# One list schedule for both phases up to the branch, second-phase pools laid over the first's one by one, and the adaLN gate summed piece by piece

## The chip, the core and the metric

The kernel runs on one core of one Trainium2 chip. The core has five engines with an instruction queue each: TensorE (PE, matrix products), VectorE (DVE), ScalarE (ACT), GpSimd (POOL) and SyncE (SP, which here only issues transfers between memory and the core). They run side by side and wait for each other through semaphores. The metric is the device time of one execution in microseconds (us); the time of a kernel is the median of its runs.

## The reference

One decoder layer on a sequence of 4096 tokens with 1024 features. The input is normalised and modulated by an adaLN vector that is computed from a condition `c`, goes through one combined input projection into three mixers, and their outputs go through one output projection, a second norm, the adaLN gate and the residual:

```python
def _hybrid_layer(x, c_act, ada_w, ada_b, ...):
    shift, scale, gate = jnp.split(c_act @ ada_w + ada_b, 3, axis=-1)
    h = _rmsnorm(x, g_pre) * (1.0 + scale[:, None]) + shift[:, None]
    proj = h @ w_in
    aq, ak, av, ag, rkv, rg, gq, gkk, gv, gg = jnp.split(proj, ...)
    attn = _sliding_window_attention(aq, ak, av, sinks)      # 8 heads, 2 kv heads, window 128, sinks, ALiBi
    attn = attn * jax.nn.silu(ag)
    rkv = rkv + (_shift(rkv) - rkv) * mu_rkv
    rr, rk, rv = jnp.split(rkv, 3, axis=-1)
    rwkv = _rwkv7_mixer(h, rr, rk, rv, ...) * jax.nn.silu(rg)   # 4 heads, delta-rule state
    gla = _gla_mixer(h, gq, gkk, gv, ...) * jax.nn.silu(gg)     # 4 heads, chunks of 64
    y = jnp.concatenate([attn, rwkv, gla], axis=-1) @ w_out
    return x + gate[:, None] * _rmsnorm(y, g_post)
```

`shift` and `scale` are needed before the first token, `gate` only in the output stage.

## The kernel before

The sequence is cut into 16 supertiles of 256 tokens (`NT = 256`, `NS = 16`), and the program has two phases.

**Phase 1** computes the norm, the modulated h (kept as an fp16 pair of high and low part, `hT`, which is also written out to `hscr`), the GLA mixer and the RWKV-7 mixer; their outputs go to `mscr`. Per supertile it is written as generators: `stage_a` (norm, h), `stage_p` (GLA values, `pv`, and the low-rank gates, `lp`), `stage_d`, `stage_r`, `stage_k`, `stage_v` (the RWKV projections, all called `zz`), `stage_qa`, `stage_qb` and `stage_qc` (GLA products, and the RWKV triangular system) and `stage_q2`. In the triangular system `atp` holds products of RA and KB; they go through memory (`adr` to `AS`), a loop of 15 steps on VectorE (`tsc`, `TT`) inverts blocks, the result goes through memory again (`tdr` to `td`), and `Xp`, `Xq`, `X` on PE finish it into `tf`. `stage_q2` is serial: four chunks, each of `rp`, `rs`, `up`, `UV`, `sp`, `yp` and the state `Sst`, then the normalised `ysb` is transposed (`yt`). `stage_c` rewrites the weights of the second phase as high and low halves (`wscr`, `woscr`) along the way.

`stage_g` sums the gate, `silu(c) @ ada_w` for its 1024 columns. It takes 16 pieces of 128 x 4 x 128 numbers (256 KB each): SP loads a piece into the tile `hf`, GpSimd multiplies it by the condition (`scol`) and adds it up into `acc`, PE sums the partitions (`gp2`, two products of 512 columns), and the row goes to `gscr`. It is gated on the last supertile's `stage_a` and `stage_d`.

**Phase 2** is sliding attention, gates, output projection and residual. Its weights are seven pairs q0 to q6 of `wscr` (q0, q1 the queries, q2 keys and values, q3 to q6 the silu gates, products `gp` into `ag`). `stage_w` loads them, `stage_first` runs `qkv(0)`, `gates(0)`, `qkv(1)`, `stage_s(0)` is the attention of supertile 0 (scores `sc`, softmax `pr`, `ovp`), and `load_o` brings in the output weights. Then the program reads a flag, and all engines go through a branch (L1910) to a fallback that runs only if a GLA gate grew too large. After the branch come `stage_s` 1 to 15 and the output stages. Two transfers matter in the tail: `q5h` to `q6l` (weights) and `vscr`/`v_` (values of the attention).

**What sets the order.** Every instruction goes through a helper, `Lane.call` (L320, so almost every row of the profile bears this line), which records it as a step with a cost in a table of dependences. `Order.pin()` is a list scheduler over the recorded steps: it takes, engine by engine, the step that can start first, by a rank that is the place of its recording, moved by `LAG` and `URGENT`, and then fixes each engine's order by dependences. Recording order itself comes from `streams`, a list of generators with ranks, run by `emit`. `pin()` is called once, after phase 1. The steps of phase 2 up to the branch are recorded afterwards, and stand behind it in an order that follows their own priorities; which of them move in between phase 1's last steps is decided by buffers and priorities, not by the scheduler. The pools of phase 2 are allocated after phase 1's are given back, in one piece of memory.

Of the kernel before, what the change touches and what calls it, by code (L numbers as in the profile page):

```python
# [21 lines left out]
P = 128  # L22
D = 1024
T = 4096
NT = 256
NS = T // NT
# [3 lines left out]
LN2 = math.log(2.0)  # L30
GATE_LIMIT = 30.0
HOP, VL, AL, PL = 0.4, 0.2, 0.2, 0.06
EXP_TABLE, LN_TABLE = 1, 2
# [13 lines left out]
class Pool:  # L47


    def __init__(self, pool, bufs, held):  # L50
        self.pool, self.bufs, self.held = pool, bufs, held

    def tile(self, shape, dt, bufs=None, **kw):
        t = self.pool.tile(shape, dt, **kw) if bufs is None else self.pool.tile(shape, dt, bufs=bufs, **kw)
        self.held[t.tensor.name] = self.bufs if bufs is None else bufs
        return t

# [7 lines left out]
class Order:  # L65
# [3 lines left out]
    def __init__(self, tc):  # L69
        self.tc, self.held, self.masks, self.lag, self.urgent = tc, {}, {}, 0, 0  # L70
        self.steps = []
        self.wrote, self.read, self.users, self.slots, self.known = {}, {}, {}, {}, set()

    def pool(self, pool, bufs=1):
        return Pool(pool, bufs, self.held)

# [22 lines left out]
    def note(self, eng, name, outs, ins, func, r):  # L99
# [21 lines left out]
        elif e == "SP":  # L121
            st.bytes = math.prod(ins[0].shape) * SIZE[ins[0].dtype]
            kb = st.bytes / 1024
            st.occ = 0.47
            st.lat = next((t for k, t in ((8, 1.9), (32, 2.0), (128, 2.3), (256, 2.6), (512, 3.5)) if kb <= k), 4.8)
# [84 lines left out]
    def forget(self):  # L210

        self.steps = []
        for table in (self.wrote, self.read, self.users):
            table.clear()

    def pin(self):
# [167 lines left out]
def hybrid_kernel(ctx, tc, x, vecs, rows, adaw, w1, wl, w2, wo, w2aug, a2, gk2, cst, ctr, ctg, abias, out):  # L384
    nc = tc.nc
# [6 lines left out]

    def pool_of(at, name, bufs=1, **kw):
        return model.order.pool(at.enter_context(tc.tile_pool(name=name, bufs=bufs, **kw)), bufs)

# [87 lines left out]

    wa = pool_of(ctx, "wa", 1)
    sp_ = pool_of(ctx, "shared", 1)

# [137 lines left out]
    with ExitStack() as p1:  # L624

        wk1 = [pool_of(p1, f"work1{n}", 1) for n in "abcd"]
        pp = pool_of(p1, "c1p", 1)
        order = (("hf", "gl", "b1", "zs", "gw", "cgc", "bl", "gk1s", "zl0", "zl1", "zl2", "ch", "cl", "cs"),
                 ("zb0", "zb1", "zb2", "ta", "ep", "em", "b2", "KB"),
# [341 lines left out]
        def stage_g(_):  # L971

            yield [("a", NS - 1), ("w", NS - 1)]
            for g in range(2):
                acc = wt([P, 4, P], "acc", 1, tag="gw")
                for n in range(4):
                    for h in range(2):
                        aw = wt([P, 4, P], "hf", 2)
                        SP.dma_start(aw, adaw[8 + 2 * g + n // 2, :, 4 * h : 4 * h + 4, (n % 2) * P : (n % 2 + 1) * P])
                        yield [aw]  # L980
# [528 lines left out]

        streams((9, "l", stage_l, None), (11, "g", stage_g, None))  # L1510
        for i in range(NS):
# [10 lines left out]
    w2k, pp, wg, w2m, w2p, w2o, wb = [pool2(n) for n in ("work2k", "c2p", "wg", "work2m", "work2p", "work2o", "wb")]  # L1522
    pools = {"q": w2k, "kT": w2k, "vt": w2k, "v4": w2k, "mxa": w2m, "mxb": w2m, "pr": w2p, "yv": w2o, "sm1": w2o}

# [56 lines left out]
    def qkv(i):  # L1581
# [25 lines left out]
        for n in range(2):  # L1607
# [42 lines left out]
    def stage_s(i):  # L1650
# [3 lines left out]
        q, kT, v4 = f["q"], f["kT"], f["v"]  # L1654
        yield [q, kT, "at", "sq"]

        vblk = [F[i - 1]["v"][1] if i > 0 else None, *v4]
        mx = f["mx"] = wt([P, 4, NT], "mxa", 2)
        for a in range(2):
# [4 lines left out]
            for jp in range(2):  # L1664
                for kv in range(2):
                    sc = pst(("at", "sq")[kv], "sc").rearrange("p (j n) -> p j n", j=2)
                    for jj in range(2):
# [8 lines left out]
                if jp == 0:  # L1676
                    yield ["at", "sq"]
            nm = st.tile([P, 8], F32, tag="nm", name="nm")
# [20 lines left out]
            for kv in range(2):  # L1699
# [8 lines left out]
            ov = [pst(tag, "ovp")[:, 0:P].rearrange("p (j n) -> p j n", j=4) for tag in tags]  # L1708

# [10 lines left out]
            for n in range(4):  # L1720
                S.copy(mx[:, 0:4, a * P + 32 * n : a * P + 32 * n + 32], ov[n])
            yield ["at", "sq"]

# [166 lines left out]
    for t, n in tiles_o:  # L1890
        load_o(t, n)


    flag = nc.values_load(fi[0:1, 0:1], min_val=0, max_val=1)
# [157 lines left out]
```

## Time and profile before

| what | value |
|---|---|
| median of 3 runs | 2154.26 us (2151.35 to 2157.72) |
| profiled execution, its own time | 2149.78 us |
| its span | 2148.0 us |
| mean granted clock of TensorE | 0.988 |
| instructions | 59214 |
| GpSimd busy | 199.9 us (9%) |

Read the profile like this: first which engine is busy through the span, then where its digit falls, then the waits in these places, then what the releaser was doing at that time. A supertile of phase 1 takes some 62 us, and phase 2 begins in earnest at the branch at about 1165 us.

### The profile page before, as it was taken

The numbers are of one execution on the slowest core, as the hardware profiler recorded it, in microseconds if no ns is written. First come the engines' busy times: TensorE is split into PE (matmuls) and PEld (weight loads), VectorE is DVE, ScalarE is ACT, GpSimd is POOL, SyncE is SP. The second block draws the span as 40 slices with busy tenths as digits, with TensorE's granted clock in tenths as the row PEclk, the third lists the DMA queues.
The fourth block names the chain that finished last, engine by engine and source line by source line (L and its number), as shares of the span: only waits on it lengthen the run. The fifth ranks groups of instructions, "written<-read, shape, count | busy, mean of one in ns | idle before, by whom it ended". The sixth has DMA issues, their size and how long they took to land. (4 is left out here: it accounts for less than half of the span.)

```text
span 2148.0 us, 59214 instructions
## 1 busy us (share of the span) xinstructions
PE 2037.3 (95%) x23735; PEld 1600.4 (75%) x23735; DVE 1626.2 (76%) x5204; ACT 1144.5 (53%) x2741; POOL 199.9 (9%) x404
## 2 busy tenths in 40 slices
PE   4999999999999999999878999999999999999996
PEld 4778878888888887777657667777777777777773
DVE  6677677787777689887756888777778877777876
ACT  3966666667676667754324444434344444444442
POOL 0011111110111110112700000000000000000000
PEclk9999999999999999999989999999999999999998
DMA  9232322232323134422515343433343333334341
GB/s 316 91 108 82 93 77 84 71 96 84 120 78 107 42 108 123 126 83 62 172 53 179 128 160 106 135 103 111 115 135 121 121 121 111 115 115 141 110 132 69
DMA packets 187243, 241.80 MB, mean 113 GB/s; under 512 B 52160, under 2 KB 145874, under 8 KB 182740
## 3 DMA queue, kind: packets, MB, share of 16 engines
q1 hardware_dynamic: 185220, 236.76, 34.1%
q8 instruction: 188, 3.08, 0.6%
q10 hardware_dynamic: 1744, 1.21, 0.2%
q14 instruction: 91, 0.75, 0.1%
HBM read 177.08 MB, written 60.82 MB: 111 GB/s over the span
## 5 line engine op out<-in xcount | busy, mean ns | idle before, releaser
L320 PEld LDWEIGHTS <-mtp 128*128 128x128 f16 x1344 | 130.7, 98 | 143.9 <-issue 5.1
L320 PE MATMUL op<-o,mtp 128*128 128x512 f16 x768 | 174.2, 380 | 0.0
L320 ACT ACTIVATE pr<-pr,nm,lsc 128x256 f32<-128x256 f32 (+1 forms) x256 | 149.2, 585 | 38.6 <-DVE nm L320 38.6
L320 PE MATMUL op<-ov,mtp 128*128 128x512 f16 x576 | 146.0, 384 | 2.1 <-ACT mtp L320 2.1
L320 PEld LDWEIGHTS <-hT 128*128 128x128 f16 x1536 | 117.4, 99 | 22.9 <-issue 4.4
L320 DVE TENSOR_TENSOR yv<-op,yv 128x512 f32<-128x512 f32 x112 | 75.2, 683 | 57.6 <-PE op L320 40.6
L320 DVE CUSTOM_DVE_ANT_0 pr<-sc,ab,sinks 128x256 f32<-128x256 f32 (+1 forms) x256 | 108.1, 476 | 13.3 <-PE sc L320 8.4
L320 ACT ACTIVATE mtp<-yv,oi 128x1024 f16<-128x1024 f32 x32 | 36.6, 1144 | 126.3 <-DVE yv L320 124.8
L320 ACT ACTIVATE ag<-gp,gh 128x512 f32<-128x512 f32 x64 | 43.7, 682 | 108.2 <-PE gp L320 108.2
L320 PE MATMUL pv<-gvh,hT 128*128 128x272 f16 x512 | 99.8, 284 | 1.4 <-DVE kg L320 1.3
L320 DVE SCALAR_TENSOR_TENSOR ag<-ag,gp 128x512 f32<-128x512 f32 x64 | 43.8, 684 | 71.4 <-ACT ag L320 71.3
L320 POOL COPY kT<-kT 128x512 f16<-128x512 f16 x15 | 9.8, 652 | 896.5 <-DVE kT L320 896.5
L320 PE MATMUL zz<-hT,kh 128*128 128x256 f16 x512 | 92.7, 273 | 0.0
L320 PE MATMUL qp<-hT,q1h 128*128 128x256 f16 x512 | 88.9, 277 | 2.7 <-issue 2.3
L320 PE MATMUL gqk<-hT,gqkh 128*128 128x256 f16 x512 | 87.5, 273 | 4.0 <-DVE zb L320 3.3
L320 PE MATMUL zz<-hT,rh 128*128 128x256 f16 x512 | 89.5, 278 | 0.0
L320 PE MATMUL lp<-hT,Lh 128*128 128x256 f16 x512 | 89.3, 273 | 0.1
L320 PE MATMUL qp<-hT,q0h 128*128 128x256 f16 x512 | 85.4, 273 | 2.7 <-DVE ag L320 2.3
L320 PE MATMUL zz<-hT,vh 128*128 128x256 f16 x512 | 87.8, 273 | 0.0
L320 PE MATMUL gp<-hT,q3h 128*128 128x256 f16 x512 | 87.2, 276 | 0.1
L320 PE MATMUL gp<-hT,q5h 128*128 128x256 f16 x512 | 86.7, 273 | 0.0
L320 ACT ACT_TABLE_LOAD x65 | 83.4, 1283 | 5.3 <-DMA sinks<-in_rows 4.2
(428 smaller groups left out, 6146.8 us busy)
## 6 DMA issues: line engine op xcount, KB each, us to landing
ov<-woscr SPq DMA_DIRECT2D x96, 512.0 KB, 4.1
xt<-in_x SPq DMA_DIRECT2D x16, 1024.0 KB, 4.9
hscr<-hT SPq DMA_DIRECT2D x16, 1024.0 KB, 4.7
hT<-hscr SPq DMA_DIRECT2D x16, 1024.0 KB, 4.9
out<-yv SPq DMA_DIRECT2D x32, 512.0 KB, 2.9
x<-in_x SPq DMA_DIRECT2D x30, 512.0 KB, 3.9
cs<-in_w SPq DMA_DIRECT2D x112, 128.0 KB, 2.2
v<-vscr SPq DMA_DIRECT2D x128, 64.0 KB, 3.0
```

The costliest lines, as they stand in the source:

```text
L320: r = f(*args, **kw)
```

## The change

1. `pin()` is no longer called after phase 1 but after `load_o`, just ahead of the branch, so that phase 1, `stage_w`, `stage_first`, `stage_s(0)` and the loads of the output weights are one list schedule.
2. The second phase's pools are laid over the first's one by one. `Pool` knows its users, and the first use of a second-phase tile depends on every step that used the first-phase pools it lies on (`w2k` over pool a; `c2p` and `work2m` over a and b; `wg`, which holds q5 and q6, over b and c; `work2o` over b, c and d; `wb`, the output weights, over c, d and `c1p`). `work2p` (`pr`) becomes a pool of its own. The scratch for dynamic transfers is made smaller (`dynamic_dma_scratch_size=1024`).
3. `stage_g` has rank 0.5 instead of 11, four groups instead of two, each gated on the `stage_a` of supertile 4, 6, 8 or 10, with tiles of its own (`gaw`, one buffer, and `gac`). In the planner's cost its loads are 5 us later.
4. For `qkv(0)`, `qkv(1)` and `stage_s(0)` other PSUM banks are used (`pj` in place of `mq`; `tr` and `m` in place of `at` and `sq`; `at`, `pj` in place of `y`, `mq`).

The core of the diff:

```diff
@@ class Pool / Order
-    def __init__(self, pool, bufs, held):
-        self.pool, self.bufs, self.held = pool, bufs, held
+    def __init__(self, pool, bufs, held, owner, over):
+        self.pool, self.bufs, self.held, self.owner, self.over, self.used = pool, bufs, held, owner, over, []
...
-            st.lat = next((t for k, t in ((8, 1.9), ..., (512, 3.5)) if kb <= k), 4.8)
+            st.lat = next((t for k, t in ((8, 1.9), ..., (512, 3.5)) if kb <= k), 4.8) + self.late
...
         for t, tensor in tiles.items():
+            if t in self.owner:
+                self.owner[t].used.append(k)
             if t not in self.known:
                 self.known.add(t)
+                for p in self.owner[t].over if t in self.owner else ():
+                    for j in p.used:
+                        need(j)
@@ stage_g
-            yield [("a", NS - 1), ("w", NS - 1)]
-            for g in range(2):
-                acc = wt([P, 4, P], "acc", 1, tag="gw")
-                for n in range(4):
+            for g in range(4):
+                yield [("a", GATE_FROM + 2 * g)]
+                acc = wt([P, 2, P], "gac", 1)
+                for n in range(2):
                     for h in range(2):
-                        aw = wt([P, 4, P], "hf", 2)
-                        SP.dma_start(aw, adaw[8 + 2 * g + n // 2, ...])
+                        aw = wt([P, 4, P], "gaw", 1)
+                        model.order.late = 5.0
+                        SP.dma_start(aw, adaw[8 + g, ...])
+                        model.order.late = 0.0
...
-                yield [acc, "m"]
+                yield [acc, "m", ("a", GATE_FROM + 2 * g + 1)]
-                PE.matmul(gp2, ones, acc.rearrange("p n c -> p (n c)"), start=True, stop=True)
-                gr = wt([P, 512], "gr", 1, tag="ta")
-                V.tensor_copy(gr[0:1, :], gp2[0:1, :])
-                SP.dma_start(gscr[:, g * 512 : (g + 1) * 512], gr[0:1, :])
+                row = acc.rearrange("p n c -> p (n c)")
+                PE.matmul(gp2[:, 0:NT], ones, row, start=True, stop=True)
+                V.tensor_copy(row[0:1, :], gp2[0:1, 0:NT])
+                SP.dma_start(gscr[:, g * NT : (g + 1) * NT], row[0:1, :])
@@ end of phase 1
-        streams((9, "l", stage_l, None), (11, "g", stage_g, None))
+        streams((9, "l", stage_l, None), (0.5, "g", stage_g, None))
...
         emit()
-        model.order.pin()
-    def pool2(name):
-        return pool_of(ctx, name, 1, reuse_waits="tile")
+    def pool2(name, over):
+        return pool_of(ctx, name, 1, over, reuse_waits="tile")
-    w2k, pp, wg, w2m, w2p, w2o, wb = [pool2(n) for n in (...)]
+    w2k, pp, w2m, wg, w2o, wb = [pool2(n, [wk1[m] for m in over]) for n, over in (
+        ("work2k", (0,)), ("c2p", (0, 1)), ("work2m", (0, 1)), ("wg", (1, 2)), ("work2o", (1, 2, 3)), ("wb", (2, 3, 4)))]
@@ qkv, stage_s
-        yield ["mq"]
-        vp = mq("vp")
+        yield ["mq" if i > 1 else "pj"]
+        vp = mq("vp") if i > 1 else pjt("vp")
...
-        yield [q, kT, "at", "sq"]
+        sct = ("at", "sq") if i else ("tr", "m")
+        yield [q, kT, *sct]
...
-            tags = ("tr", "m", "y", "mq")
+            tags = ("tr", "m", "y", "mq") if i else ("tr", "m", "at", "pj")
@@ after load_o
+    model.order.pin()
     flag = nc.values_load(fi[0:1, 0:1], min_val=0, max_val=1)
```

The order that results is shown at three places. The first is GpSimd's queue at the start of the program, before and then after (`bl`, `zl` and `zs` belong to phase 1; `gaw` and `gac` are the gate's tiles).

```order
18 L320 COPY TT<-tdelta 128x128
19 L320 MEMSET bl 128x1
20 L320 COPY zl_861<-zs 128x2
21 L320 MEMSET zs 128x2
22 L320 COPY zl_991<-zs 128x2
```

```order
18 L329 COPY TT<-tdelta 128x128
19 L329 ISA
20 L329 TENSOR_TENSOR gaw<-gaw,scol 128x512
21 L329 TENSOR_TENSOR gaw<-gaw 128x256
22 L329 TENSOR_TENSOR gac<-gaw 128x128
...
33 L329 TENSOR_TENSOR gac<-gaw 128x128
34 L329 MEMSET bl 128x1
35 L329 TENSOR_TENSOR gaw<-gaw,scol 128x512
36 L329 COPY zl_864<-zs 128x2
```

Four pieces, 14 operations, now stand ahead of phase 1's first `bl`, and the fifth begins right behind it; their loads stand in SP's queue among the first weights. The other pieces stand between the GpSimd operations of later supertiles, and none is left in the last ones.

The second is SP's queue at the end of phase 1, before and then after (`td` is the second trip of the last triangular system, `mscr<-ysb` the RWKV output).

```order
415 L320 DMA gscr<-gr 1x512
416 L320 DMA mscr<-osb 128x512
417 L1894 TENSOR_LOAD fi
418 L1894 ISA x2
419 L320 DMA q5h<-wscr 128x2048
420 L320 DMA q5l<-wscr 128x2048
421 L320 DMA q6h<-wscr 128x2048
422 L320 DMA q6l<-wscr 128x2048
423 L320 DMA mscr<-ysb 128x512
```

```order
429 L329 DMA td<-tdr 16x8x16 x8
430 L329 DMA vscr<-vt 128x2x128
431 L329 DMA v_18076<-vscr 32x4x128 x4
432 L329 DMA v_18077<-vscr 32x4x128
433 L329 DMA mscr<-ysb 128x512
434 L329 DMA v_18077<-vscr 32x4x128 x3
435 L329 DMA q5h<-wscr 128x2048
436 L329 DMA q5l<-wscr 128x2048
437 L329 DMA q6h<-wscr 128x2048
438 L329 DMA q6l<-wscr 128x2048
439 L329 DMA mscr<-ysb 128x512
```

The loads of q5 and q6 now stand behind the value loads of the attention.

The third is PE's queue in the chunks of the last `stage_q2`, before (first chunk) and then after (the last chunk).

```order
10826 L320 MATMUL up<-rs,tf_461 64x64 x4
10827 L320 LDWEIGHTS q3l
10828 L320 MATMUL gp<-hT,q3l 128x256
10829 L320 LDWEIGHTS q3h
10830 L320 MATMUL gp<-hT,q3h 128x256
10831 L320 LDWEIGHTS q3h
10832 L320 MATMUL gp<-hT,q3h 128x256
10833 L320 LDWEIGHTS q3l
10834 L320 MATMUL gp<-hT,q3l 128x256
10835 L320 MATMUL yp<-UV,AT 64x64
10836 L320 MATMUL sp<-UV,BK 64x64 x4
```

```order
11167 L329 MATMUL up<-rs,tf_464 64x64 x4
11168 L329 MATMUL yp<-UV,AT 64x64
11169 L329 MATMUL sp<-UV,BK 64x64 x4
11170 L329 MATMUL yp<-UV,AT 64x64 x3
11171 L329 LDWEIGHTS q5h
11172 L329 MATMUL gp<-hT,q5h 128x256
11173 L329 LDWEIGHTS q5h
11174 L329 MATMUL gp<-hT,q5h 128x256
11175 L329 MATMUL ovp<-pr,v_18076 64x128 x8
11176 L329 MATMUL yt<-ident,ysb 128x128 x4
11177 L329 LDWEIGHTS q5l
```

Before, matmuls of the gate products q3 and q4 stand between the steps of a chunk. Now q3 and q4 stand ahead of the chain's last part, and between its steps there are scores and `ovp` of supertile 0; the rest of q5, then q6, and `qkv(1)` follow behind `yt`.

More of the change, by code (lines that the diff above doesn't have):

```diff
@@ L31 @@
 GATE_LIMIT = 30.0
+GATE_FROM = 4
 HOP, VL, AL, PL = 0.4, 0.2, 0.2, 0.06
@@ L55, in tile @@
         self.held[t.tensor.name] = self.bufs if bufs is None else bufs
+        self.owner[t.tensor.name] = self
         return t
@@ L69, in __init__, with pool @@
     def __init__(self, tc):
-        self.tc, self.held, self.masks, self.lag, self.urgent = tc, {}, {}, 0, 0
+        self.tc, self.held, self.masks, self.lag, self.urgent, self.late, self.owner = tc, {}, {}, 0, 0, 0.0, {}
         self.steps = []
         self.wrote, self.read, self.users, self.slots, self.known = {}, {}, {}, {}, set()
-    def pool(self, pool, bufs=1):
-        return Pool(pool, bufs, self.held)
+    def pool(self, pool, bufs=1, over=()):
+        return Pool(pool, bufs, self.held, self.owner, over)
     def region(self, ap):
@@ L124, in note @@
             st.occ = 0.47
-            st.lat = next((t for k, t in ((8, 1.9), (32, 2.0), (128, 2.3), (256, 2.6), (512, 3.5)) if kb <= k), 4.8)
+            st.lat = next((t for k, t in ((8, 1.9), (32, 2.0), (128, 2.3), (256, 2.6), (512, 3.5)) if kb <= k), 4.8) + self.late
         elif e == "Activation":
@@ L214, in forget @@
             table.clear()
+        for p in self.owner.values():
+            p.used.clear()
     def pin(self):
@@ L391, in hybrid_kernel, with pool_of @@
     SP = Lane(model, nc.sync, *LANES[4])
-    def pool_of(at, name, bufs=1, **kw):
-        return model.order.pool(at.enter_context(tc.tile_pool(name=name, bufs=bufs, **kw)), bufs)
+    def pool_of(at, name, bufs=1, over=(), **kw):
+        return model.order.pool(at.enter_context(tc.tile_pool(name=name, bufs=bufs, **kw)), bufs, over)
     cp = pool_of(ctx, "const", 1)
@@ L484, in hybrid_kernel @@
     wa = pool_of(ctx, "wa", 1)
+    w2p = pool_of(ctx, "work2p", 1)
     sp_ = pool_of(ctx, "shared", 1)
@@ L627, in hybrid_kernel @@
         pp = pool_of(p1, "c1p", 1)
-        order = (("hf", "gl", "b1", "zs", "gw", "cgc", "bl", "gk1s", "zl0", "zl1", "zl2", "ch", "cl", "cs"),
+        wk1.append(pp)
+        order = (("hf", "gl", "b1", "zs", "gw", "cgc", "bl", "gk1s", "zl0", "zl1", "zl2", "ch", "cs", "gaw", "gac"),
                  ("zb0", "zb1", "zb2", "ta", "ep", "em", "b2", "KB"),
@@ L1665, in stage_s @@
                 for kv in range(2):
-                    sc = pst(("at", "sq")[kv], "sc").rearrange("p (j n) -> p j n", j=2)
+                    sc = pst(sct[kv], "sc").rearrange("p (j n) -> p j n", j=2)
                     for jj in range(2):
@@ L1676, in stage_s @@
                 if jp == 0:
-                    yield ["at", "sq"]
+                    yield [*sct]
             nm = st.tile([P, 8], F32, tag="nm", name="nm")
@@ L1705, in stage_s @@
                     V.transpose(pT[kv].rearrange("p j n -> p (j n)"), pr[kv].rearrange("p j n -> p (j n)"))
-            tags = ("tr", "m", "y", "mq")
+            tags = ("tr", "m", "y", "mq") if i else ("tr", "m", "at", "pj")
             yield [*pT, *v4, *tags]
-            ov = [pst(tag, "ovp")[:, 0:P].rearrange("p (j n) -> p j n", j=4) for tag in tags]
+            ov = [pst(tag, "ovp", 2 if tag == "pj" else 1)[:, 0:P].rearrange("p (j n) -> p j n", j=4) for tag in tags]
             lo = 4 if first else 0
@@ L1721, in stage_s @@
                 S.copy(mx[:, 0:4, a * P + 32 * n : a * P + 32 * n + 32], ov[n])
-            yield ["at", "sq"]
+            yield [*sct]
     def block(i, n):
@@ L2044 @@
     arrays = _layout(inputs)
-    nc = _bacc.Bacc("TRN2", target_bir_lowering=False, num_devices=1)
+    nc = _bacc.Bacc("TRN2", target_bir_lowering=False, num_devices=1, dynamic_dma_scratch_size=1024)
     args = [nc.dram_tensor(n, a.shape, mybir.dt.from_np(a.dtype), kind="ExternalInput").ap() for n, a in arrays.items()]
```

3 lines of the change are left out of this document (1 added, 2 removed).

## The prediction

> **What bounds the kernel now.** I read the page's busy times and its 40 slices first, then the windows, the waits of PE, and the timeline where the waits are.
>
> ```profile
> PE 2037.3 (95%) x23735; PEld 1600.4 (75%) x23735; DVE 1626.2 (76%) x5204; ACT 1144.5 (53%) x2741; POOL 199.9 (9%) x404
> PE   4999999999999999999878999999999999999996
> ```
>
> TensorE (PE) is busy for 95% of the span; its digits fall at the start, in slices 20 to 22 (about 1020 to 1180 us, the seam between the phases) and at the end. The windows size these places (columns: length, then busy time and instructions of PE, PEld, DVE, ACT and POOL, granted clock, DMA share, GB/s).
>
> ```profile
> 0.00:50.00 50.00, 23.64 (x106) 22.84 (x106) 34.85 (x129) 16.75 (x36) 3.18 (x19) 1.00 0.93 311
> 600.00:800.00 200.00, 197.16 (x2727) 164.65 (x2724) 154.70 (x559) 135.45 (x313) 27.72 (x63) 1.00 0.27 83
> 1020.00:1040.00 20.00, 17.78 (x201) 15.07 (x202) 13.66 (x33) 12.62 (x23) 12.64 (x22) 0.91 0.78 250
> 1040.00:1060.00 20.00, 17.62 (x322) 12.87 (x321) 13.08 (x24) 2.41 (x8) 15.51 (x22) 1.00 0.47 151
> 1060.00:1080.00 20.00, 14.58 (x190) 11.17 (x189) 18.30 (x84) 3.28 (x9) 12.40 (x19) 1.00 0.21 60
> 1080.00:1100.00 20.00, 15.22 (x267) 10.30 (x267) 12.24 (x35) 8.20 (x17) 2.19 (x5) 0.74 0.43 139
> 1100.00:1120.00 20.00, 17.87 (x237) 12.82 (x238) 6.47 (x29) 4.12 (x12) 0.00 (x0) 0.83 0.01 2
> 1120.00:1140.00 20.00, 18.08 (x195) 15.97 (x193) 11.19 (x54) 8.42 (x25) 0.00 (x0) 1.00 0.41 124
> 1140.00:1160.00 20.00, 17.59 (x252) 14.90 (x247) 14.11 (x44) 9.95 (x32) 0.61 (x1) 1.00 0.54 189
> 1160.00:1180.00 20.00, 16.75 (x154) 14.14 (x151) 10.98 (x29) 6.07 (x13) 0.00 (x0) 0.83 0.45 157
> ```
>
> In mid-phase PE stands idle 2.84 us of 200. At the seam it is busy 135.5 us of 160, so 24.5 us are idle, and part of the busy time ran below full clock: 17.78 x 0.09 + 15.22 x 0.26 + 17.87 x 0.17 + 16.75 x 0.17 = 11.4 us. No more than some 36 us can be won there, less what the serial chain of the last supertile forces. Two waits of PE between 1000 and 1170 us (total, times, longest) and the moments of that chain (start, length):
>
> ```profile
> PE yt L320 <- DVE ysb L320: 4.1, 3, 2.9
> ...
> PE atp L320 <- DVE RA L320: 2.4, 1, 2.4
> ```
>
> ```profile
> 998.08 0.38 PE L320 MATMUL zz<-hT,kh 128*128 128x256 f16 x2
> ...
> 1055.33 0.28 PE L320 MATMUL atp<-RA,KB 64*64 64x128 f32 x2
> ...
> 1062.91 0.17 DVE L320 TENSOR_TENSOR tsc<-TT,AS 128x16 f32<-128x16 f32 x1
> ...
> 1066.37 0.94 DVE L320 TENSOR_TENSOR tsc<-TT,AS 128x48 f32<-128x48 f32 x1
> ...
> 1068.36 0.25 DVE L320 TENSOR_TENSOR tsc<-TT,AS 128x56 f32<-128x56 f32 x1
> ...
> 1079.89 0.28 DVE L320 TENSOR_REDUCE TT<-tsc 128x8 f32<-128x128 f32 x1
> ...
> 1093.11 1.08 PE L320 MATMUL Xp<-D,ATm 32*32 32x32 f32 x64
> ...
> 1102.88 0.47 PE L320 MATMUL up<-rs,tf 64*64 64x64 f32 x2
> ...
> 1104.25 0.69 PE L320 MATMUL up<-rs,tf 64*64 64x64 f32 x6
> ...
> 1109.46 0.45 PE L320 MATMUL up<-rs,tf 64*64 64x64 f32 x8
> ...
> 1112.76 0.45 PE L320 MATMUL up<-rs,tf 64*64 64x64 f32 x8
> ...
> 1117.14 0.45 PE L320 MATMUL sp<-UV,BK 128*64 128x64 f32 x8
> ...
> 1119.53 0.38 PE L320 MATMUL gp<-hT,q4h 128*128 128x256 f16 x2
> ...
> 1122.80 0.38 PE L320 MATMUL gp<-hT,q4h 128*128 128x256 f16 x2
> ...
> 1124.40 0.66 PE L320 MATMUL yt<-ident,ysb 128*128 128x128 f32 x4 [0.79 <-DVE ysb L320]
> ...
> 1167.85 0.26 PE L320 MATMUL vp<-q2l,hT 128*128 128x128 f16 x1 [3.25 <-PEq L1910]
> ```
>
> I start a clock at 998.08, where the order is still the same in both kernels. The last atp ends at +57.5, Xp of supertile 15 begins at +95.0, its first up stands at +104.8, the last sp at +119.1, yt at +126.3, and PE reaches the branch 3.25 us before 1167.85, at +166.5. 30 matmuls from 1119.53 to 1122.80 give 0.109 us each, so a product of 48 takes 5.2 us. Counting every PE instruction of the order at such rows, the work from 998.08 to the branch is about 128 us; the other 38 are idle and slow clock.
>
> **The seam in the new order.** Two things change. First, the gate leaves: no hf load, no GpSimd sum, no gp matmul of 512 columns stands there any more. Its GpSimd groups (busy, mean ns, then idle before) and what they do to VectorE:
>
> ```profile
> L320 POOL TENSOR_TENSOR hf<-hf,scol 128x512 f32<-128x512 f32 x16 | 17.3, 1083 | 22.4 <-DMA hf<-in_adaw 22.3
> L320 POOL TENSOR_TENSOR hf<-hf 128x256 f32<-128x256 f32 x16 | 12.1, 758 | 0.7
> L320 POOL TENSOR_TENSOR acc<-hf 128x128 f32<-128x128 f32 x16 | 7.8, 490 | 11.2 <-DVE Gst L320 10.4
> L320 POOL TENSOR_TENSOR hf<-hf,acc 128x128 f32<-128x128 f32 x8 | 4.0, 496 | 0.5
> ```
>
> ```profile
> 1017.06 2.18 POOL L320 TENSOR_TENSOR hf<-hf,scol 128x512 f32<-128x512 f32 x2 [4.43 <-DMA hf<-in_adaw]
> ...
> 1017.23 0.90 DVE L320 TENSOR_TENSOR nwt<-yr 128x8 f32<-128x8 f32 x1
> 1018.16 0.17 DVE L320 SCALAR_TENSOR_TENSOR nwt<-nwt,ve 128x8 f32<-128x8 f32 x1
> 1018.36 0.90 DVE L320 SCALAR_TENSOR_TENSOR yr<-nwt,yr 128x8 f32<-128x8 f32 x1
> ...
> 1022.22 0.66 PE L320 MATMUL yt<-ident,ysb 128*128 128x128 f32 x4 [2.94 <-DVE ysb L320]
> ```
>
> The sum is 41.2 us of GpSimd, 2.6 us for each of 16 pieces. Under the 2.18 us of two multiplies, two 8-column operations of VectorE take 0.90 instead of 0.17 us, 0.67 us of stretch per us of GpSimd, and the ysb chain arrives 2.94 us late at PE, which then runs at a clock of 0.91 over the window. With the gate gone I strike out this wait with its clock loss (2.9 + 1.6) and the atp wait (2.4), since RA is a victim of the same kind. The Trainium skill's page "GPSIMD Engine Reference", section 1 (row "SBUF interfaces"), says that GpSimd shares its SBUF interfaces with VectorE and contends with VectorE instructions that have two SBUF inputs; 0.90 against 0.17 us agrees, and the rule speaks against the new places as much as the old.
>
> Second, the PE order. Before the last atp it now has 53.6 us of work (48.3 before), so that atp ends near +55. From it to Xp(15) lead VectorE's loop (1062.91 to 1080.17, 17.3 us), its transfers and transposes, 37.5 us in all. In the loop a step of 48 columns took 0.94 where one of 56 took 0.25; four of the fifteen are stretched so, which is worth some 2 us, and about 35 remain without GpSimd. PE has 32.8 us of work there (the rest of q0, then q1, vp, q3 and most of q4) against 22.4 before, so it fits below the chain, and Xp(15) comes at about +90, 5 us earlier.
>
> From there it is less well filled: the loads of q5 and q6 now stand behind the v loads, and between Xp(15) and the end only sc, ovp and two gp matmuls are left, where before q3 and q4 filled the gaps. Xp to up takes 9.8 us and up to sp 14.3 us in both. For s(0)'s softmax operations on VectorE and for small matmuls at a slow clock I add 2.5: the first chunk, in a window with a clock of 0.83, took 1109.46 - 1104.25 = 5.2 us against 3.3 for the next, so the bounds are 0.5 (all hidden) and 7 (1.9 more in each, every wait exposed). sp to yt stays 7.2 (0.79 of it shows as a wait before, the rest was covered by q4), and nothing covers it now. Then stand q5, q6, kp, q0, q1, ovp, vp: 29.5 us of work, and 1.7 us for a slow start. Sum: 90 + 9.8 + 14.3 + 2.5 + 7.2 + 29.5 + 1.7 = 155. Against 166.5 that is 11.5 less, and about 1.3 us of vp and sc that stood behind the branch now lie before it: **-13**, with bounds -8 and -17. The branch itself (3.25 us) stays.
>
> **Start-up.** In the order of SP two gate pieces precede the last adaLN weights, a third follows them and a fourth and fifth come with the second and third xt. The transfer queue is full there (0.93, 311 GB/s): 256 KB cost 0.84 us, two of them 1.7. GpSimd's 2.6 us for each fall on VectorE's accumulation, whose operations read two SBUF tiles; at 0.67 per us that is 3.5 for two pieces. Low bound 0.5 (both lie beside waits that are there anyway), high 5 (their sum). The first pv stands at
>
> ```profile
> 55.52 0.41 PE L320 MATMUL pv<-gvh,hT 128*128 128x272 f16 x1
> ```
>
> and all PE work waits for that, so the delay is paid whole. I take **+2.5**.
>
> **Mid-phase.** 11 or 12 pieces, 30 us of GpSimd, make 20 us of stretch by the same rate, spread over some 400 us in which VectorE is idle for about a quarter (154.70 of 200). PE has no slack of its own (197.16 of 200), so whatever reaches it is paid, at bounds of 0 and 20. I take **+2.5**, nearer to hidden because at 1000 to 1020 us, where the damage was seen, VectorE was also serving the last supertile's chain. The eight extra transfers of 256 KB stand in a window with a DMA share of 0.27 and cost nothing; without that room they would cost 0.84 each. GpSimd's own masks and copies (qb, ATm, zl) queue behind a piece for up to 2.6 us; POOL is 14% busy there, and these are included. A gp matmul of 256 columns replaces one of 512 at the same cost per column.
>
> Sum: -13 + 2.5 + 2.5 = **-8 us**. The profiled execution took 2149.78 us (span 2148.0), so it would take 2141.8; it lies 4.5 below the median of 2154.26 of the three runs (2151.35 to 2157.72), and on that median the forecast is 2146.3.
>
> **The rivals.**
> (B) *More is won.* VectorE's slack swallows the contention (start +1, mid 0) and the seam gives 17: -16, 2138. For it: 25% slack. Against it: the unfilled chain.
> (C) *Given back.* Seam -9, start +4, mid +5: 0, 2154. For it: PE's missing filler beside the chain and the full queue at the start.
> (D) *Slower: the ysb stall repeats.* In each of supertiles 4 to 10 a piece falls on the normalisation before yt; a wait of 2.9 and 1.6 of slow clock in each of seven is +31, with the start +2.5 and the seam -13 about +21, 2175. From three of the seven the kernel is slower than before, from four measurably. For it: the 2.94 us seen once; against it: 16 pieces near the seam produced one such wait. The Trainium skill's "TensorE: Matmul & The Clock Gate", Part 1, has a free-running window of about 3.4 us after which an idle PE is set to half rate; by that rule a wait of 2.94 us need not cost any clock, and D would be +10. The granted clock of 0.91 between 1020 and 1040 us shows that this one did.
> (E) *It does not do what it says.* Gate pieces run at the start instead of at supertiles 4 to 10, since the condition on supertile 4 holds back only the recording of steps. If all the early ones hit the critical accumulation (+5) and the chain has its high price (seam -8), mid +3.5 leaves +0.5, 2155.
>
> **How the numbers follow.** Chances: forecast (-8, own range -3 to -13) 0.45, B 0.20, C 0.15, D 0.13, E 0.07. A measurement of this kernel tells about 0.3%, 6.5 us, from no change. The forecast lies 0.27 beyond that bound and 0.18 inside it; with B, faster is 0.47. C and E lie within, 0.18 together of their 0.22, making the same 0.36; D and their rest are slower, 0.17. The range reaches from 2135, below B, to 2162, which leaves out most of D.
>
> **What would show it.** Right: no gate work on POOL after about 750 us; at 1017 to 1027 us no yt wait near 3 us and no clock below 1.00; the TT loop near 15 us; Xp(15) about 90 us after the first zz<-kh of supertile 15; the branch about 155 us after it; the first pv at 57 to 59 us; PE idle no more than 4 us per 200 in supertiles 4 to 10. Wrong: yt or atp waits of 2 to 3 us in most of those supertiles (D); a first pv beyond 61 us (E); chunks of 5 us all along the last chain, or PE waiting for q5 (C). The forecast falls if the branch comes later than +160 or if mid-phase windows show over 5 us of new PE idle time.

## The result, and the profile after

The changed kernel is slower. It took 2168.97 us in the median of six runs (2166.01 to 2174.24), the kernel before 2154.37 beside it; the ratio is 1.0072 with a 95% interval of 1.0053 to 1.0092. On the chips of the experiments the kernel before took 2163.5 to 2165.7 us in its medians, so below whole times are given as ratios to the kernel before on the same chip. The change run there again had 1.0037 (1.0018 to 1.0056).

The profiled execution took 2170.09 us, span 2168.3, which is 20.3 more than the profiled span before; the medians lie 14.6 apart, since the profiled execution before (2149.78) was as quick as the quickest of its runs (2149.76 to 2157.72). These are the windows of the changed kernel (columns as above: length; busy time of PE, PEld, DVE, ACT, POOL; granted clock, DMA share, GB/s):

```profile
0.00:50.00 50.00, 19.98 (x94) 19.35 (x95) 36.63 (x124) 16.67 (x35) 8.60 (x25) 0.89 0.89 293
600.00:800.00 200.00, 194.28 (x2589) 160.53 (x2587) 147.29 (x527) 130.13 (x316) 34.95 (x73) 0.98 0.28 86
1040.00:1060.00 20.00, 19.58 (x169) 17.12 (x168) 13.96 (x67) 13.13 (x28) 1.09 (x5) 1.00 0.50 147
1060.00:1080.00 20.00, 18.87 (x355) 14.58 (x354) 14.35 (x30) 5.52 (x11) 5.86 (x9) 0.91 0.45 154
1080.00:1100.00 20.00, 19.85 (x261) 15.23 (x255) 14.55 (x55) 4.48 (x12) 1.57 (x3) 1.00 0.05 10
1120.00:1140.00 20.00, 13.66 (x268) 10.92 (x266) 10.01 (x44) 6.94 (x27) 1.60 (x4) 0.61 0.19 69
1140.00:1160.00 20.00, 15.57 (x131) 11.57 (x129) 9.69 (x48) 3.60 (x8) 0.00 (x0) 0.54 0.04 14
```

The seam is filled as planned up to 1120 us: PE is busy for 18.9 us or more of every 20 between 1020 and 1120, its longest wait from 1020 to 1100 is one of 0.96 us for RA (2.9 for ysb and 2.4 for RA before), and only at 1060 to 1080 is the clock below 1.00 (0.91). Then come 40 us in which PE is busy for 29.2 at a clock of 0.61 and 0.54. And in 600 to 800 us, far from the seam, PE lost 2.9 us against before. The moments that the prediction had named, on the timeline of PE:

```profile
60.12 0.41 PE L329 MATMUL pv<-gvh,hT 128*128 128x272 f16 x1
...
1023.85 0.38 PE L329 MATMUL zz<-hT,kh 128*128 128x256 f16 x2
...
1117.89 0.75 PE L329 MATMUL Xp<-D,ATm 32*32 32x32 f32 x64
...
1128.47 1.10 PE L329 MATMUL up<-rs,tf 64*64 64x64 f32 x8 [0.61 <-DVE tf L329]
...
1145.93 0.69 PE L329 MATMUL sp<-UV,BK 128*64 128x64 f32 x8
...
1153.15 1.12 PE L329 MATMUL yt<-ident,ysb 128*128 128x128 f32 x4 [3.66 <-DVE ysb L329]
...
1189.91 0.37 PE L329 MATMUL sc<-kT,q 128*128 128x256 f16 x1 [2.79 <-PEq L1927]
```

| stretch | before | after | difference | forecast |
|---|---|---|---|---|
| start to first pv | 55.52 | 60.12 | +4.6 | +2.5 |
| first pv to zz<-kh of the last supertile | 942.6 | 963.7 | +21.2 | +2.5 |
| from there to the branch | 166.5 | 163.3 | -3.2 | -11.5 |
| behind the branch | 983.4 | 981.2 | -2.2 | -1.3 |

The last row is the span less the moment at which PE reaches the branch. The four differences sum to the 20.3 us. They are those of two single executions; how far such stretches vary from one execution to the next is shown below. So the loss is in mid-phase, and the gain at the seam came to about a quarter (3.2 of 11.5).

### The profile page after: what moved, and what is told of

Read it like the earlier page. It is cut to its first block, busy times and chain, and to the rows that moved or that the text cites. A ratio compares the mean times of both kernels' runs of the same rounds, so it can differ in the third digit from the quotient of the medians.

```text
span 2168.3 us, 59231 instructions
## 1 busy us (share of the span) xinstructions
PE 2046.4 (94%) x23739; PEld 1608.1 (74%) x23739; DVE 1632.2 (75%) x5206; ACT 1146.2 (53%) x2741; POOL 201.2 (9%) x404
## 5 line engine op out<-in xcount | busy, mean ns | idle before, releaser
L329 PE MATMUL sc<-kT,q 128*128 128x256 f16 (+1 forms) x512 | 72.6, 275 | 17.2 <-DVE m L329 13.1
```

Of the source, the lines that this page charges most:

```text
L329: r = f(*args, **kw)
```

## The experiments

**Which part costs: a square of four.** The change has two large parts that can be had alone. e1 is the change with `stage_g` as it was, e2 the kernel before with the new one.

```diff
-        streams((9, "l", stage_l, None), (0.5, "g", stage_g, None))
+        streams((9, "l", stage_l, None), (11, "g", stage_g, None))
```

This is the line of e1, against the changed kernel; the function `stage_g` of the kernel before goes with it. e2 exchanges the same two things the other way round in the kernel before.

> The change, but with the gate's sum in its old form and place (two groups, gated on the last supertile). Theory 1 (the early gate pieces cost the time, through GpSimd's work beside VectorE): first pv at 55.5 us again, the last supertile's first zz<-kh near 998 us instead of 1023.9, and the whole at 2148 to 2156 us, level with before or a little faster. Theory 2 (one list schedule for both phases deals phase 1's steps out worse, whatever the gate does): the last supertile still begins past 1010 us and the whole stays above 2162.

> The kernel before, with only the gate's new form and rank. Theory 1: the last supertile begins some 20 to 26 us later than before (1018 to 1024 us), the tail is shorter by the contention that has left it (5 to 10), the whole at 2164 to 2174 us. Theory 2: phase 1 runs nearly as before, the whole at 2146 to 2156.

e1: 0.9971 (0.9955 to 0.9987). e2: 1.0041 (1.0021 to 1.0060). With the change itself at 1.0037 on these chips and 1.0072 in its own comparison, the early gate costs 0.4% in the old schedule and 0.7% or more in the new one, whereas the single list schedule alone wins 0.3%. In e1 the last supertile starts at 1004.75 us, in e2 at 1027.28. Up to there the matmuls of e1 stand in the order of the kernel before (6 of some 12,290 differ in the traces), and those of e2 in the order of the change (5 differ), while the two orders differ from each other in some 2,600. So the early gate's steps gave mid-phase its new order, and the single list schedule did not. Of what mid-phase loses the seam gives something back once the gate is out of it: in e2 the branch is reached 154.1 us after the last supertile's first zz<-kh, where the changed kernel needs 163.3 and two executions of the kernel before 166.5 and 174.5.

**The gate's work or its order?** The planner places every instruction anew when the gate's steps stand elsewhere. e4 and e8 keep that new order (up to the last supertile about 250 and 46 matmuls stand otherwise than in the change) and take most of the work out of it, by telling the planner the old size (`pretend`) and running a few columns; e4 keeps the loads, e8 cuts them too.

```diff
 e8, in stage_g (e4 likewise, with the whole load)
+                        model.order.late, model.order.pretend = 5.0, 4 * P
-                        SP.dma_start(aw, adaw[8 + g, :, 4 * h : 4 * h + 4, n * P : (n + 1) * P])
+                        SP.dma_start(aw[:, 0, 0:4], adaw[8 + g, :, 4 * h, n * P : n * P + 4])
...
+                        G.tensor_tensor(aw[:, 0, 0:4], aw[:, 0, 0:4], scol[:, 4 * h : 4 * h + 4], op=ALU.mult)
+                        G.tensor_tensor(aw[:, 0, 0:2], aw[:, 0, 0:2], aw[:, 0, 2:4], op=ALU.add)
 in Order.note, engine Pool
+            n = self.pretend or n
```

> The change with the gate's GpSimd multiplies and adds cut to one column of 128 (the planner is told the old cost, so nearly all instructions keep their places); the gate's values are left out of the computation by it. Theory 1: about 2.2 of 2.6 us of GpSimd work per piece go, and with them most of the delay: the last supertile begins at 1000 to 1008 us, the whole at 2148 to 2156. Theory 2 (the order itself, or the loads): the last supertile still begins past 1015 us, the whole stays above 2162.

> The kernel before, for a trace of this chip beside the others. First pv near 55.5 us, the last supertile's first zz<-kh 942 to 950 us later; every theory expects that.

> The change, on the chip of the experiments beside it. Every theory expects a ratio near 1.007 and the last supertile 964 to 972 us behind the first pv.

> The change with the gate hollowed out: its loads cut from 256 KB to 2 KB, its GpSimd multiplies and adds to 2 or 4 columns, while the planner is told the old sizes, so that all but some 30 of 27,000 PE instructions keep their places; the gate's values are left out of the computation by it. Theory 1 (the work costs: GpSimd beside VectorE, or the loads): nearly all of the delay goes, the last supertile stands 944 to 952 us behind the first pv, the ratio is 0.990 to 0.998. Theory 2 (the order in which phase 1 was dealt out costs): it still stands 957 us or more behind the first pv, the ratio stays at 1.000 or above.

e4: 1.0010 (0.9986 to 1.0034), with the last supertile 965.5 us behind the first pv, which is theory 2's number, not theory 1's. e8: 0.9997 (0.9984 to 1.0010), and 961.3 us: more than theory 1 allowed. b0, a0 and e8 ran on one chip, and a finer look is possible there: the last `lp<-hT,Ll` of supertile 4 and the start of the last supertile, first in the kernel before, then in the change, then in e8, each from its timeline of PE.

```profile
55.87 0.41 PE L320 MATMUL pv<-gvh,hT 128*128 128x272 f16 x1
...
305.41 0.27 PE L320 MATMUL lp<-hT,Ll 128*128 128x256 f16 x1
...
1005.29 0.38 PE L320 MATMUL zz<-hT,kh 128*128 128x256 f16 x2
```

```profile
60.58 0.41 PE L329 MATMUL pv<-gvh,hT 128*128 128x272 f16 x1
...
306.88 0.27 PE L329 MATMUL lp<-hT,Ll 128*128 128x256 f16 x1
...
1029.11 0.38 PE L329 MATMUL zz<-hT,kh 128*128 128x256 f16 x2
```

```profile
57.11 0.41 PE L331 MATMUL pv<-gvh,hT 128*128 128x272 f16 x1
...
307.23 0.27 PE L331 MATMUL lp<-hT,Ll 128*128 128x256 f16 x1
...
1018.38 0.38 PE L331 MATMUL zz<-hT,kh 128*128 128x256 f16 x2
```

From supertile 4 to the last one the three took 699.9, 722.2 and 711.2 us. So taking out the work saves 11.0 us there (722.2 - 711.2, nearly the same order), and 11.3 (711.2 - 699.9) remain for the order and for what e8 still runs: its small gate operations keep GpSimd busy for 12.0 us in that stretch, against 29.1 in a0. The 11.0 is thus rather a low bound for the work and the 11.3 a high one for the order.

Single executions differ by several us even in one order. All traces of these runs and of those below, by the order of their matmuls up to the last supertile (equal but for 20 matmuls or fewer in the first two rows; d5, of which more below, differs from e8 in 27; e4, whose order is farther off, is left out):

| order and work | traces | first pv to last supertile | that `lp` of supertile 4 to last supertile |
|---|---|---|---|
| old order (before, b0, e1, e1b, c4 twice, c5, c7) | 8 | 942.6 to 950.2 | 695.4 to 700.2 |
| change's order, full gate (after, a0, e2, e6) | 4 | 963.7 to 971.1 | 716.0 to 722.2 |
| change's order, hollow gate (e8, d5) | 2 | 955.6 and 961.3 | 708.8 and 711.2 |

The ranges do not meet, so there is a cost that goes with the work and one that stays without most of it, each known to within some 5 us. Whole runs bear out the first: the median of e8 lies 7.6 us under that of a0, the start included. Neither theory was right alone.

Whether the delay at the start is absorbed later is not settled: of the 4.7 us between b0 and a0 at the first pv 1.5 are left at supertile 4, but of the 4.6 in the first comparison 5.1 stand there (302.71 and 307.80 us).

What the waits look like in the order of e8, without most of the gate's work, and beside it in the kernel before on the same chip (waits of PE, 300 to 990 and 300 to 980 us: total, times, longest):

```profile
PE Xp L331 <- DVE T L331: 3.5, 3, 1.3
PE atp L331 <- DVE RA L331: 2.8, 3, 1.4
...
PE cgp L331 <- DVE gl L331: 1.2, 1, 1.2
```

```profile
PE ot L320 <- DVE osb L320: 3.3, 4, 1.4
PE tp L320 <- ACT hf L320: 1.5, 2, 1.2
```

In the new order it is the RWKV triangular chain (RA, T) that PE waits for, between 420 and 740 us; its two rows sum to 6.3 us in e8 and to 0.5 in b0. The waits are single microseconds, but they come with clock: from the first pv to the last supertile the trace shows 24 us at half clock in e8, 27 in the change, 14 in b0. At most half of that is lost.

**Is every new order worse?** d3 and d4 are e1 with a trifle added that moves the deal: four copies of a row on VectorE, or seven copies behind GpSimd memsets. The scheduler runs all of these in the first 25 us, so mid-phase has a new order and no new work. d5 is e8 with the planner told the true sizes; by the traces its order came out almost as that of e8 (27 of the first 12,290 matmuls differ, against some 2,600 from e1), so it is the deal of e8 once more and not another one.

```diff
 d3, in stage_a
+            if i in (4, 6, 8, 10):
+                nod = st.tile([P, NT], F32, tag="nod", name="nod", bufs=1)
+                V.tensor_copy(nod[0:1, :], vt[0:1, 0:1].to_broadcast([1, NT]))
 d4, in stage_a
+            if 4 <= i <= 10:
+                nod = st.tile([P, NT], F32, tag="nod", name="nod", bufs=1)
+                for _ in range(3):
+                    G.memset(nod, 0.0)
+                V.tensor_copy(nod[:, 0:P], ident)
```

> The kernel of e1_gate_last (gate in its old place) with one thing added: VectorE copies one row of 256 numbers into an unused tile in supertiles 4, 6, 8 and 10, as the early gate does. That alone moves 556 of the first 10,018 PE rows. Theory 2 (any new deal of phase 1's list schedule costs some 10 us against before's, whatever gave rise to it): the last supertile stands 956 us or more behind the first pv (949.05 in e1), the ratio 0.4% or more above e1's 0.9971. Rival (a deal is as good as another, the loss of e8 comes from waits on the gate's own instructions): 946 to 952 us, a ratio of 0.995 to 0.999.

> As d3, another draw: in supertiles 4 to 10 a copy of 128 columns on VectorE behind three memsets of 256 columns on GpSimd, 786 rows moved. Theory 2: 956 us or more again from first pv to the last supertile. Rival: 946 to 954 us (the added work itself is 7 x 0.2 us of VectorE and 7 x 0.9 of GpSimd).

> e8 (the gate hollowed out, its values left out) with the planner told the true small sizes, so that it deals phase 1 out anew: 742 of the first 10,018 PE rows stand differently from e1's. If every deal but before's costs, the last supertile stands 957 us or more behind the first pv, as in e8 (961.3); if only some do, 946 to 953 us is as likely, as in d3.

From first pv to the last supertile d3 took 943.3 us, d4 956.7 and d5 955.6, where the eight traces of the old order took 942.6 to 950.2. In d3 and d4 some small matmuls of the chain stand behind that mark that stood before it (116 and 80, more than half and a fifth of them `atp`); at the 0.068 us of an `atp` (16 in 1.09 us) that is an estimated 8 and 5 us, so that this mark flatters both. The whole times are the better measure here. d3: 0.9977 (0.9960 to 0.9993), the same as e1 (0.9971). d4: 1.0041 (1.0022 to 1.0059), 0.7% or some 15 us more than e1, of which 9 stand ahead of the first pv and about 6 behind it. d5: 0.9976 (0.9956 to 0.9996). So one new deal cost nothing, another some 6 us, and that of the change about the 11 above at most. Theory 2 as it stood falls: a new order can be as good as the old one. Which feature of an order makes the chain late was not found. At the start of d4 the first pv stands at 64.75 us; VectorE stood 13.6 us behind the GpSimd memsets that its copies waited for.

**The pieces at the start.** e3 makes the condition real: before its first load each group writes one column from `hT` of supertile 4, 6, 8 or 10.

```diff
+                        if not n and not h:
+                            G.tensor_copy(aw[:, 0, 0:1], E[GATE_FROM + 2 * g]["hT"][:, 0, 0, 0:1])
```

> The change with the gate truly held to supertiles 4, 6, 8 and 10 (one column of its tile is first written from that supertile's hT, so the load has to wait). The pieces at the start go: both theories expect the first pv within 0.7 us of before's. Theory 1: the delay after that is that of 16 pieces instead of 12, the last supertile 960 us or more behind the first pv. Theory 2: this is another draw of the order, and anything from 943 to 975 us can come; 952 or less would be evidence for it against theory 1.

First pv at 55.68 us, so the 4.6 us are the early pieces. It is their work on GpSimd more than their loads: the first pv stands at 57.24 us in e4, which keeps the loads, and at 57.11 in e8, which does not. Yet the whole of e3 is 1.0045 (1.0027 to 1.0062), as slow as the change, and the last supertile stands 975.4 us behind the first pv. Theory 1's number came. The order up to there is nearly the change's (41 matmuls differ), so this was not another draw: the 4 to 12 us above the four traces of the change's order go with the four more pieces in mid-phase, as far as one trace can tell.

**The seam.** The planner takes q5 and q6 (pool `wg`, over b and c) for blocked until all users of c are done, and `cd` and `em0`, two tiles of a few columns in c, are read to the end of the last chain. e6 moves them to d, in the change; e1b does so in e1.

```diff
-                 ("qg", "kg", "egp", "egm", "vg", "c2", "kt", "cd", "em0"))
+                 ("qg", "kg", "egp", "egm", "vg", "c2", "kt"))
```

> The change with the two small tiles cd and em0, which the last supertile's chain reads to its end, moved from pool c to pool d, so that the planner no longer takes q5 and q6 (pool wg over b and c) for blocked until that chain ends. Theory Q (the tail gave only 3 of 13 us since q5 and q6 stand behind the chain, PE idles and its clock is halved there): PE is busy over 17 of 20 us in the windows of the chain, the branch comes 150 to 157 us after the last supertile's first zz<-kh instead of 163.3, the whole at 2158 to 2164. Rival (the chain on VectorE and the late yt bound the tail whatever fills PE): 161 us or more, 2167 to 2171.

> e1_gate_last with cd and em0 moved to pool d as in e6. Theory Q: phase 1 as in e1, q5 and q6 can fill the last chain, so the branch comes 5 to 15 us earlier than e1's +175.2, part of it is given back behind the branch by the late output weights; the ratio is 0.992 to 0.996. Rival: the gate's own row copy (pool b) and its GpSimd work keep the end of phase 1 as it is, 0.997.

e6: 1.0016 (0.9997 to 1.0035), some 0.2% below a0, which is within their intervals. Theory Q had the chain and the branch right, the rival had the whole time (2168.76 us). Its windows at the chain and behind it:

```profile
1120.00:1140.00 20.00, 16.60 (x349) 13.40 (x349) 12.90 (x55) 8.17 (x28) 1.61 (x4) 1.00 0.42 139
1140.00:1160.00 20.00, 19.75 (x284) 16.15 (x283) 13.21 (x67) 10.15 (x33) 0.00 (x0) 1.00 0.01 2
1160.00:1180.00 20.00, 12.75 (x204) 11.12 (x202) 10.82 (x25) 5.83 (x13) 0.77 (x1) 0.98 0.49 163
1180.00:1200.00 20.00, 12.52 (x84) 9.72 (x83) 8.10 (x23) 5.02 (x12) 0.00 (x0) 0.76 0.74 254
```

```profile
1179.89 0.59 PE L329 MATMUL gp<-hT,q3h 128*128 128x256 f16 x2 [5.49 <-PEq L1927]
...
1199.18 0.59 PE L329 MATMUL mp<-mss,ones 128*128 128x2 f32 x2 [7.48 <-ACT mtp L329]
```

The chain is filled and the clock stays at 1.00 through it; the branch is reached 143.8 us after the last supertile's start (1030.57), 20 less than in a0. But 12 of the 20 come back behind the branch: PE waits 5.49 us there and 7.48 us for `mp`, which sums the squares of the first supertile's mixer outputs. The ten loads of output weights stand in SP's queue behind the store of the last ysb, so they start at 1169 us however early PE is (DMA share 0.01 before that, 0.74 after); behind them stand the loads of `x` (1187.07) and of those mixer outputs, `mxb` (1187.71), and VectorE stands 9.57 us for `x` ahead of its work on `mxb`, for which `mp` waits. The chain itself, Xp to the last sp, took 28.3 us in e6 at full clock and 28.0 in the change at half clock: the clock did not set its length, which is mostly VectorE's: the softmax operations on `pr` of supertile 0 take 7.7 us of VectorE between these two marks in the change, and in e2, where none stand there, the chain takes 18.2. e1b: 0.9977 (0.9957 to 0.9997), no better than e1, the rival's number. In its trace the branch comes 169.3 us after the last supertile's first zz<-kh, against 175.2 in e1, and behind the branch nothing is lost (981.8 us against 981.0); that the medians do not show these 6 us may be the spread of single executions (166.5 and 174.5 for the kernel before) and stays open.

**The gate on PE.** c4 takes the gate off GpSimd: `scol` is the weight, a piece the moving tensor, one row comes out, and 64 fp32 passes cost 15.7 us of PE, where some 10 had been expected. It stands in the old place at the end of phase 1, where PE has gaps, and leaves phase 1's order alone. c7 is c4 without the move of `cd` and `em0`; c5 is the kernel before with this gate.

```diff
+                for h in range(2):
+                    aws = [wt([P, 2, NT], "hf", 2) for _ in range(2)]
...
+                    for k in range(4):
+                        PE.matmul(gp2[0:1, 0:NT], scol[:, 4 * h + k : 4 * h + k + 1], aws[k // 2][:, k % 2, :], start=(k == 0), stop=(k == 3))
```

> e1b with the gate summed on PE (scol as the weights, 32 products of 256 columns, one row out) in the old place, and no GpSimd work for it at all. Theory: the last supertile's VectorE chain runs without GpSimd beside it (no yt wait near 3 us, a loop of about 15 us), and PE's some 10 us for the products fall in the gaps of the chain; the ratio is 0.988 to 0.994. Rival: PE is the bound at the seam too, so its 10 us are paid in full and the ratio is 0.996 or above.

> The kernel before, with only the gate's sum moved from GpSimd to PE in its old place at the end of phase 1. If c4's gain comes from the gate, the ratio is 0.990 to 0.995 here too; if it needs the one list schedule and the early q5 and q6, 0.996 to 1.000.

> c4 without the move of cd and em0: the change's one list schedule, the gate on PE at the end. By the gate alone 0.991 to 0.996; if the early q5 and q6 carry c4's gain, 0.997 or above.

> c4 again beside the two others, on one chip with them: a ratio of 0.990 to 0.995, the branch some 160 us after the last supertile's first zz<-kh.

| kernel | ratio to before | interval |
|---|---|---|
| c5: before, gate on PE | 0.9971 | 0.9950 to 0.9991 |
| c7: change, gate on PE | 0.9911 | 0.9883 to 0.9939 |
| c4 again: c7 with early q5, q6 | 0.9907 | 0.9878 to 0.9936 |
| c4, first time | 0.9926 | 0.9900 to 0.9951 |

c7 beats both kernels by about 0.9% and more. The early q5 and q6 add nothing that can be told. The gate alone (c5) gives 0.3%, the list schedule alone (e1) 0.3%, both together 0.9%. The sum of the two would be 0.6%, and the intervals do not exclude it, so that the schedule gains more once no GpSimd work lengthens the last chain is a guess. The groups and waits of c4 again, 1000 to 1170 us:

```profile
L329 PE MATMUL gp<-hf,scol 128*1 128x256 f32 x64 | 15.7, 378 | 1.7 <-DMA hf<-in_adaw 1.4
```

```profile
PE sc L329 <- PEq L1922: 2.8, 1, 2.8
PE kp L329 <- ACT BK L329: 1.5, 1, 1.5
PE gp L329 <- DMA hf<-in_adaw: 1.4, 1, 1.4
```

No wait of PE above 1.5 us is left there but the branch's own.

## Why the prediction was wrong

**Mid-phase, the step that failed.** The prediction took +2.5 us for 11 or 12 pieces between bounds of 0 and 20 and chose near the low one, because VectorE idles for a quarter of the time and because the damage it had seen stood beside the last supertile's chain. The runs showed +21.2 in the first comparison. It consists of two things. At least some 11.0 us from supertile 4 on go with the gate's work (a0 against e8), in the middle of the bounds: a mean idle share of VectorE says nothing of the few chains in which it is the last to arrive. And up to 11.3 stay when most of the work is gone (e8 against b0); for these, the order, the sum had no term at all. It treated mid-phase as unchanged but for added work, though some 2,600 of the 12,290 matmuls ahead of the last supertile stood elsewhere and the order of the rows was there to be compared. Why this order is slower is not known beyond the waits for T and RA. Rival D, the one that had the sign, built its +21 on yt stalls of 2.9 us in each of seven supertiles. Its total was near the 20.3 of the profiles, which is luck, for its mechanism was not there: no yt wait in mid-phase reaches 1.5 us, the waits are for T and RA.

The rate of 0.67 us of stretch for each us of GpSimd was too high as well. From the first pv to the last supertile VectorE is busy for 720.6 us in the kernel before, 731.9 in the change and 724.4 in e8, with 33.8 us of gate operations on GpSimd in the change: some 10 us of stretch instead of 20. The trace agrees in this with the rule cited from the Trainium skill, "GPSIMD Engine Reference", section 1, that GpSimd shares its SBUF interfaces with VectorE. No run tells this contention from the gate's place in GpSimd's queue, and the rule says nothing of the order. (The "eight" extra transfers of the prediction are 11 or 12, one for each piece; their price was put at nothing, and no run isolates it.)

**Start-up.** +2.5 was forecast, +4.6 came at the first pv, near the upper bound of 5; e3 shows that the early pieces make it. Whether "the delay is paid whole" is open: by supertile 4 one pair of traces has 1.5 us of 4.7 left, the other 5.1 of 4.6.

**The seam.** -11.5 was forecast up to the branch, -3.2 came. Right was that the gate's stalls vanish (at 1020 to 1100 us no wait is above 0.96 us, and the clock is below 1.00 in one window only, 0.91). From the last atp to Xp 35.3 us came, where 35 was said; but Xp stands at +94.0 instead of +90 (95.0 before), because that atp ended at +58.7 and not near +55. Short too was the chain behind it: 9.8 + 14.3 + 2.5 = 26.6 was said, 28.0 came, and behind yt 34.0 us instead of 31.2. So the terms were each a little too small, 4.0 + 1.4 + 2.8 = 8.2, and at least one price was shared: with PE unfilled its clock fell to 0.54, and the work behind yt began slowly. e2 shows what was there to win: without the gate's work there and with the old schedule of the seam, 154.1. The single schedule added the softmax of supertile 0 to VectorE's part of the chain (18.2 us from Xp to the last sp in e2, 28.0 here).

**Rival C** was right on the missing filler beside the chain, and its +4 at the start came; the full queue it gave for that did not make it, since e4 with the whole loads starts as early as e8. **Rival E** had the place and the price (+5) of the early pieces right; its +3.5 for mid-phase was as far off as the forecast's +2.5.

## What to carry to other kernels

When a scheduler deals out the work, a change to a few steps changes the order everywhere, and this can cost as much as the work itself: compare the order far from the edit, and measure the new order with the work hollowed out. A filler's engine counts as well as its place: moved to an earlier place on GpSimd, the same sum cost 0.4% and more; left in its old place but moved to PE, it was worth 0.3% in the old schedule (c5) and 0.6% in the new one (c7 against e1), even though PE is the bound engine. One trace of each kernel is not enough for effects of this size: eight of the same order spread over 7.6 us. And an early release of one buffer pays only as far as the next thing in the same queue, here the output weights behind a store, and the next inputs behind those.

## What the runs showed of the hardware that was not expected

The granted clock fell to half for 34 us in one piece while PE was still busy for 29.2 of 40 us with small matmuls (the windows 1120 to 1160 of the changed kernel), though no single wait in the first 25 of them exceeded 2.3 us; the longest, 3.66 us, came last. "TensorE: Matmul & The Clock Gate" of the Trainium skill, Part 1, speaks of idle windows of about 3.4 us and of a clock set by how busy PE has been recently; the trace agrees with the second, since here sparse work was enough.

The median of the same program was 2154.4 us in the first comparison and 2163.5 to 2165.7 in the sessions of the experiments, on three chips; that is 0.5%, as much as the effects studied. On one of these chips alone its executions spread from 2151.54 to 2169.17 us. In the first profile the seam of the kernel before took 166.5 us, in b0 174.5, and b0 had 20 us of half clock at 1052 us that the first did not have.
